# A Strassen-form FFN on one core: the order of its down preparation, and who makes its token block sums

## The chip, the cores and the metric

The kernel runs on one core of one Trainium2 chip. The core has TensorE (matmul; in the profile PE for matmuls, PEld for weight loads), VectorE (DVE), ScalarE (ACT), GpSimd (POOL) and SyncE (SP), which issues the DMAs. The metric is the time in microseconds (us) of one execution on the device; lower is better.

## The reference

One encoder layer is applied to two independent inputs of 1024 tokens x 1024 channels, with the same weights, and in the kernel the first input's pass ("trunk" 0) runs ahead of the second's (trunk 1). Only the FFN matters here:

```python
x = norm_1(h); h = h + concat(attention(x), rg_lru(x)) @ w_out     # w_out 1024 x 1024
xn = rms_norm(h, norm_ffn_g)
g, u = split(xn @ w_gate_up)          # w_gate_up 1024 x 5632
h = h + (silu(g) * u) @ w_down        # w_down 2816 x 1024
y = rms_norm(h, final_norm_g)         # meta tokens dropped
```

All is float32.

## The kernel before

**Exact products from rounded ones.** A float32 operand is split into a high part, its cast to float32r (ScalarE), and a low part, the operand minus its high part (VectorE or GpSimd). A product is then three matmuls (`mm3`): high x high, high x low, low x high.

**Seven products instead of eight.** Gate/up and down are computed in the Strassen-Winograd form: tokens, inner dimension and outputs are cut in two, and seven products of sums of blocks take the place of eight. So ahead of the matmuls stand block sums of the operands, and behind them additions of the results.

**Block sums of the tokens** (`x_side`, `sums`). The normalised token tiles `x2n` are taken in four blocks q of 2 x 128 tokens. Block q has quarters b11, b21, b12, b22, and needs T3 = b22 - b12, T1 = b12 - b11 and T2 = b22 - T1 = T3 + b11. T2 and T3 lie in the tile `t23` ("t" in the trace), T1 overwrites b12 (in `x2n`). TensorE transposes the blocks into PSUM (`tp`), ScalarE and VectorE split them into `xB`, `xT`, `xH`. For blocks 0 to 2 GpSimd makes all sums, for block 3 VectorE. `x_side` is a generator that is stepped between pieces of the output projection (`op`), while the last tiles of `h` are made and normalised: an ACT square, two small GpSimd operations (`ms`, `rs`) and one VectorE multiply for each tile.

**The down stage.** For each trunk it has seven products in the order P1, P2, P4, P5, P7, P6, P3, each in NC = 11 units of 12 matmuls (`dn_unit`): four token blocks q by three matmuls, into four PSUM banks that a product fills over its 11 units. A unit needs two operand tiles `wop`: `sop` (activations, tiles aA, aB, aC, aD, aS, aV) and `top` (weights, tiles `wraw` from HBM or `trun`). `prep_dn` makes the sums that its product asks for and ScalarE's two casts; `prep_dn_lo` makes the two low parts, that of `top` on VectorE and that of `sop` on GpSimd. Of sums, P1 and P3 have none; P2 and P7 have one on VectorE; P5 has two on VectorE; P4 has one on VectorE and one whose engine alternates (VectorE for even units, GpSimd for odd ones), besides a copy on ScalarE; P6 has one on VectorE and two of which one is VectorE's and one GpSimd's.

Operand tiles come from a ring of seven slots, so that at unit n the units n, n+1 and n+2 may hold tiles. Raw weight tiles have four slots; `load` issues the DMA of an item on SyncE's queue when the item four places ahead of it was given up by its low part (`freed`).

Every engine executes its instructions in the order in which the program issues them. For each unit n, `prep(n)` is issued first: the low parts of unit n+1 (`lows(n + 2)`), then sums and casts of unit n+2, then `lows(n + 1)`, which finds nothing left in the steady state. Then come the unit's matmuls, with at most two additions of the product before, `h += bank`, which VectorE reads from PSUM (`h<-h,dn` in the trace): after blocks q = 1 and q = 3, until the list `adds` is empty. A product leaves 16, 4, 4, 8, 8, 12 or 4 additions, in the order of the products. Behind trunk 0's P3 the first steps of trunk 1 are mixed in.

All instructions are recorded in the helper at L118, so the rows below are told apart by their tiles.

Of the kernel before, what the change touches and what calls it, by code (L numbers as in the profile page):

```python
# [12 lines left out]
ALU = mybir.AluOpType  # L13
# [23 lines left out]
NC = NHT // 2  # L37
# [207 lines left out]
def hymba_kernel(ctx, tc, ins, outs, dbg=None):  # L245
    nc = tc.nc
    plan = Plan()
    pe, act, dve, pool = (Engine(e, k, plan) for e, k in (
        (nc.tensor, "pe"), (nc.scalar, "act"), (nc.vector, "dve"), (nc.gpsimd, "pool")))
# [6 lines left out]
    def slot(tag, shape, dt=F32, name=None):  # L256
        if tag == "rope":
            return sm.tile(shape, dt, tag=tag, name=name, bufs=1)
        return sb.tile(shape, dt, tag=tag, name=name or tag)
# [168 lines left out]
    def mm3(out, lh, ll, rh, rl, first, last, more=False):  # L428

        pe.matmul(out, lhsT=lh, rhs=rh, start=first, stop=False, skip_group_check=more)  # L430
        pe.matmul(out, lhsT=lh, rhs=rl, start=False, stop=False, skip_group_check=more)
        pe.matmul(out, lhsT=ll, rhs=rh, start=False, stop=last, skip_group_check=more)
# [704 lines left out]
    def attention(T, b):  # L1137
# [324 lines left out]
        def x_alloc(n, tags, at=0, both=None):  # L1462
            tl = both if both is not None else slot(tags[0], [P, 2, 4, 512], F32R, name="x" + n)
            X[n] = (tl[:, 0], [(0, tl[:, 1])])

        def x_trans(n, q, src):
            tp = T.x_mk([P, 4, P], "tp")
            for i in range(4):
                pe.transpose(tp[:, i, :], src[:, i * P:(i + 1) * P], idf)
            hi, los = X[n]  # L1470
            qs = slice(q * P, (q + 1) * P)
            act.copy(hi[:, :, qs], tp)
            for k0, lo in los:
                k1 = k0 + lo.shape[1]
                dve.tensor_tensor(lo[:, :, qs], tp[:, k0:k1], fv(hi[:, k0:k1, qs]), ALU.subtract)
            T.x_in[n] += 1

        def x_side():
            t23 = {}

            def blocks(q):
                e, o = x2[2 * q], x2[2 * q + 1]
                return e[:, :512], e[:, 512:], o[:, :512], o[:, 512:]

            def sums(q, eng):
                b11, b21, b12, b22 = blocks(q)
                t23[q] = slot((S_CH, S_CL, "s6", "s2")[q], [P, 2, 512], name="t23")
                eng.tensor_tensor(t23[q][:, 1], b22, b12, ALU.subtract)
                eng.tensor_tensor(b12, b12, b11, ALU.subtract)
                eng.tensor_tensor(t23[q][:, 0], b22, b12, ALU.subtract)  # L1490

            def t4(q, eng):
                b21 = blocks(q)[1]
                eng.tensor_tensor(b21, t23[q][:, 0], b21, ALU.subtract)

            x_alloc("B11", T.xb[:1])
            x_alloc("T2", T.xb[1:])
            for q in range(3):
                while not {2 * q, 2 * q + 1} <= T.x2_done:
                    yield False  # L1500
                sums(q, pool)
                yield True
                x_trans("B11", q, blocks(q)[0])
                yield True
                x_trans("T2", q, t23[q][:, 0])
                yield True
            while not T.out_done:
                yield False
            x_alloc("B21", T.xa[:1])
            x_alloc("T3", T.xa[1:])  # L1510
            hi = slot("V", [P, 4, 512], F32R, name="xT1")
            X["T1"] = (hi, [(2 * i, slot(t, [P, 2, 512], F32R, name="xT1l")) for i, t in enumerate(("s7", f"wl{b}"))])
            for q in range(3):
                x_trans("T3", q, t23[q][:, 1])
                yield True
                x_trans("B21", q, blocks(q)[1])
                t4(q, pool)
                yield True
            while not {6, 7} <= T.x2_done:
                yield False  # L1520
            sums(3, dve)
            x_trans("B11", 3, blocks(3)[0])
            x_trans("T2", 3, t23[3][:, 0])
            x_trans("B21", 3, blocks(3)[1])
            t4(3, dve)
            T.x_go = True
            yield True
            x_trans("T3", 3, t23[3][:, 1])
            yield True
            for q in range(4):  # L1530
                x_trans("T1", q, blocks(q)[2])
                yield True
            hx = slot("H", [P, 2, 2, 4, 512], F32R, name="xH")
            x_alloc("T4", (), both=hx[:, 0])
            x_alloc("B22", (), both=hx[:, 1])
            for q in range(4):
                x_trans("T4", q, blocks(q)[1])
                yield True
            for q in range(4):
                x_trans("B22", q, blocks(q)[3])  # L1540
                yield True
# [54 lines left out]
        for _ in pvs:  # L1596
            pass
        pv_meta(7)
        T.side = x_side()
        for step in filler:  # L1600
            tick()
# [10 lines left out]
    def ffn_stream(T, b):  # L1612
# [12 lines left out]
        sums = {}  # L1625
# [29 lines left out]
        def load(limit=None):  # L1655

            while r_next[0] < len(items):
                i = r_next[0]
                if i >= 4 and items[i - 4][0] not in freed:
                    break  # L1660
                key, shape, parts = items[i]
                r = slot(raw_tags[i % 4], shape, name="wraw")
                for dst, src in parts:
                    sync.dma_start(out=dst(r), in_=src)
                raws[key] = r
                r_next[0] += 1
# [88 lines left out]
        def prep_dn_lo(p, c):  # L1755
            src, s, sop, top = half.pop((p, c))
            dve.tensor_tensor(top[:, 1], src, fv(top[:, 0]), ALU.subtract)
            pool.tensor_tensor(sop[:, 1], s, fv(sop[:, 0]), ALU.subtract)
            ops["dn", p, c] = (q4((sop[:, 0], sop[:, 1])), (top[:, 0], top[:, 1]))
            if p in ("P2", "P6", "P3"):  # L1760
                if c % 2 or c == NC - 1:
                    freed.add((p, c - c % 2))
            elif p in ("P4", "P5"):
                freed.add((p, c))
# [3 lines left out]
        def lows(n):  # L1768

            while n_lo[0] < min(n, T.n_prep2):  # L1770
                u = T.units[n_lo[0]]
                if u[0] == "dn":
                    prep_dn_lo(*u[1:])
                n_lo[0] += 1
            load()
# [3 lines left out]

        def prep(n):  # L1780

            lows(n + 2)
            while T.n_prep2 < len(T.units):
                u = T.units[T.n_prep2]
                need = 1 if u[0] == "gu" else 2
                out = sum(1 if x[0] == "gu" else 2 for x in T.units[n:T.n_prep2])
                if out + need > cap:
                    break
                if T.before_prep(u) is False:
                    break  # L1790
                (prep_gu if u[0] == "gu" else prep_dn)(*u[1:])
                T.n_prep2 += 1
                load()
            lows(n + 1)

        T.before_prep = lambda u: u[1:] == ("P1", 0)
        load()
        prep(0)
        T.prep_ops = prep

    def ffn(T, b, nxt):
# [9 lines left out]
        def bank(s, i, name):  # L1811
            tag = PB[s][i]
            return mk_d([P, 512], name) if tag is None else ps.tile([P, 512], F32, tag=tag, name=name)
# [113 lines left out]
        adds = []  # L1927
        banks = {}

        def add(p, q, i, l, sign, bk):  # L1930
            hs = T.h[:, 2 * q + i - 1, (l - 1) * 512:l * 512]
            dve.tensor_tensor(hs, hs, bk, ALU.add if sign > 0 else ALU.subtract)

        def dn_unit(p, c):
            n = DN.index(p)
            if c == 0:
                banks[n] = [bank(n % 2, q, "dn") for q in range(4)]
            (sh, sl), (th, tl) = ops.pop(("dn", p, c))
            for q in range(4):
                mm3(banks[n][q], sh[:, q], sl[:, q], th, tl, c == 0, c == NC - 1)  # L1940
                if q % 2 and adds:
                    adds.pop(0)()
            if c == NC - 1:
                assert not adds
                for q in range(4):
                    for i, l, sign in C[p]:
                        adds.append(lambda q=q, i=i, l=l, sign=sign, bk=banks[n][q]: (add(p, q, i, l, sign, bk), T.h_adds.add((p, q, i, l))))
# [212 lines left out]
```

## Time and profile before

| | us |
|---|---|
| median of 3 runs (lowest, highest) | 2554.81 (2551.83, 2556.84) |
| profiled execution | 2563.52 |
| its span, first to last instruction | 2561.7 |
| TensorE busy with matmuls / weight loads | 2385.7 / 2002.5 |
| VectorE / ScalarE / GpSimd busy | 1782.2 / 1168.3 / 1335.8 |
| mean granted TensorE clock | 0.97 |

Matmuls are pipelined, so a busy TensorE is not TensorE at its peak. Idle time of an engine costs something only where the chain that sets the end runs through it.

### The profile page before, as it was taken

How to read it: one execution, taken by the hardware profiler on the slowest of the kernel's cores; microseconds unless marked ns; L12 is line 12 of the kernel's file. 1: busy time of each engine (PE TensorE's matmuls, PEld its weight loads, DVE VectorE, ACT ScalarE, POOL GpSimd, SP SyncE). 2: the span in 40 equal slices, each digit the busy share in tenths (PEclk: the TensorE clock that was granted, in tenths of full speed). 3: DMA queues.
4: the chain of work that ended last, by engine and by line, in shares of the span. 5: the costliest groups of instructions: out<-in, count | busy, mean ns of one | idle time of the engine just before them, and what ended most of it. 6: DMA issues, size and time to landing. Idle time of an engine off the chain costs nothing.

```text
span 2561.7 us, 34088 instructions
## 1 busy us (share of the span) xinstructions
PE 2385.7 (93%) x12402; PEld 2002.5 (78%) x12402; DVE 1782.2 (70%) x2462; ACT 1168.3 (46%) x2083; POOL 1335.8 (52%) x1222
## 2 busy tenths in 40 slices
PE   7998999989999999998889889999799999999887
PEld 7878998867888888766677789988678888878665
DVE  6787888876555555778866778888665555557787
ACT  4456666654223232333535566666442222224434
POOL 5434766554444444445763356665544444444456
PEclk9998999989999999999999889999899999999999
DMA  5112000112222224741330130001122232247402
GB/s 137 37 35 101 19 17 18 42 66 65 76 78 82 88 74 156 271 148 38 136 128 19 35 108 18 9 18 42 66 66 74 83 91 74 83 159 276 149 30 111
DMA packets 189703, 212.77 MB, mean 83 GB/s; under 512 B 24272, under 2 KB 141008, under 8 KB 188512
## 3 DMA queue, kind: packets, MB, share of 16 engines
q1 hardware_dynamic: 189536, 210.60, 24.9%
q8 instruction: 98, 1.61, 0.3%
q14 instruction: 69, 0.57, 0.1%
HBM read 168.45 MB, written 39.85 MB: 81 GB/s over the span
## 4 chain that ended last, share of the span: by engine, by line
PE 65%; DVE 18%; ACT 6%; POOL 5%; issue 5%; DMA 1%; SPq 0%; ACTq 0%; DVEq 0%; POOLq 0%
PE gu L118 33%; PE op L118 5%; PE dn L118 5%; PE S L118 4%; PE pvo L118 4%; PE ptp L118 3%; DVE wop L118 3%; ACT wop L118 2%; PE pin L118 2%; PE qp L118 2%; DVE arena L118 2%; PE gp L118 2%; PE pg L118 1%; DVE m L118 1%; ACT arena L118 1%
## 5 line engine op out<-in xcount | busy, mean ns | idle before, releaser
L118 PE MATMUL dn<-wop 128*128 128x512 f32 x1848 | 463.4, 403 | 44.8 <-DVE wop L118 34.0
L118 PEld LDWEIGHTS dn<-wop 128*128 128x128 f32 x1848 | 340.7, 189 | 160.8 <-DVE wop L118 68.0
L118 PE MATMUL gu<-xT,wop 128*128 128x512 f32 x1408 | 371.2, 394 | 0.0
L118 POOL TENSOR_TENSOR pexp<-pexp,rsum 128x1024 f32<-128x1024 f32 x128 | 243.3, 1900 | 234.1 <-DVE rsum L118 150.7
L118 POOL TENSOR_TENSOR wop<-wraw,wop 128x512 fp32r<-128x512 f32 x176 | 230.7, 1311 | 217.0 <-ACT wop L118 217.0
L118 POOL TENSOR_TENSOR wop<-wsum,wop 128x512 fp32r<-128x512 f32 x132 | 171.7, 1301 | 269.0 <-ACT wop L118 269.0
L118 PEld LDWEIGHTS gu<-xT,wop 128*128 128x128 f32 x1408 | 264.0, 188 | 59.4
L118 PE MATMUL gu<-xB,wop 128*128 128x512 f32 x1056 | 265.5, 399 | 2.9 <-DVE xB L118 2.9
L118 ACT CAST wop<-wraw 128x512 fp32r<-128x512 f32 x264 | 162.5, 616 | 229.3 <-DVE wraw L118 159.9
L118 PE MATMUL gu<-xH,wop 128*128 128x512 f32 x1056 | 254.7, 396 | 1.7 <-DVE act L118 1.7
L118 PEld LDWEIGHTS gu<-xH,wop 128*128 128x128 f32 x1056 | 198.7, 188 | 50.5 <-issue 2.5
L118 PEld LDWEIGHTS gu<-xB,wop 128*128 128x128 f32 x1056 | 199.5, 190 | 49.0 <-DVE xB L118 3.6
L118 ACT CAST pt<-ptp 128x512 fp32r<-128x512 f32 x256 | 149.1, 586 | 127.9 <-PE ptp L118 126.7
L118 DVE TENSOR_REDUCE m<-S 128x1 f32<-128x1041 f32 x128 | 158.2, 1236 | 52.7 <-PE S L118 51.9
L118 ACT ACTIVATE pexp<-S,m 128x1041 f32<-128x1041 f32 x128 | 145.0, 1133 | 57.8 <-DVE m L118 55.1
L118 DVE TENSOR_TENSOR pt<-ptp,pt 128x512 fp32r<-128x512 f32 x256 | 168.2, 682 | 3.4 <-ACT pt L118 2.2
L118 PE MATMUL ptp<-idf,pexp 128*128 128x128 f32 x1024 | 157.0, 278 | 11.8 <-DVE pt L118 6.7
L118 PE MATMUL pvo<-pt,vst 128*128 128x256 f32 x1024 | 155.3, 295 | 3.6 <-DVE attnT L118 3.5
L118 PE MATMUL S<-kh,qs 128*128 128x348 f32 (+1 forms) x384 | 136.6, 358 | 19.3 <-ACT pexp L118 9.8
L118 ACT CAST wop<-wsum 128x512 fp32r<-128x512 f32 x132 | 81.8, 620 | 141.8 <-DVE wsum L118 141.8
L118 DVE SCALAR_TENSOR_TENSOR act<-th,act 128x512 f32<-128x512 f32 x88 | 143.8, 1634 | 3.0
L118 PEld LDWEIGHTS ptp<-idf,pexp 128*128 128x128 f32 x1024 | 126.9, 144 | 22.5 <-issue 7.8
(290 smaller groups left out, 5246.3 us busy)
## 6 DMA issues: line engine op xcount, KB each, us to landing
wraw<-in_w_gate_up SPq DMA_DIRECT2D x176, 256.0 KB, 3.5
wraw<-in_w_down SPq DMA_DIRECT2D x110, 256.0 KB, 2.8
ad<-act SPq DMA_DIRECT2D x44, 512.0 KB, 3.5
wraw<-in_w_down SPq DMA_DIRECT2D x22, 512.0 KB, 3.2
wraw<-in_w_in SPq DMA_DIRECT2D x32, 256.0 KB, 3.3
hd<-h SPq DMA_DIRECT2D x16, 512.0 KB, 5.1
h<-hd SPq DMA_DIRECT2D x16, 512.0 KB, 10.7
out<-h SPq DMA_DIRECT2D x15, 512.0 KB, 2.7
```

The lines of the kernel that those rows point to most:

```text
L118: return fn(*args, **kw)
```

## The change

Three edits. `sums`: the first difference T3 and the update of b12 are made by VectorE for each block, and T2 is made as T3 + b11 between them, by VectorE for blocks 0 and 3 and by GpSimd for blocks 1 and 2. `prep`: the low parts of unit n+1 are issued after the sums and casts of unit n+2 instead of ahead of them. `dn_unit`: the additions of the product before are spread over all 11 units of the present one, except in P3.

```diff
             def sums(q, eng):
                 b11, b21, b12, b22 = blocks(q)
                 t23[q] = slot((S_CH, S_CL, "s6", "s2")[q], [P, 2, 512], name="t23")
-                eng.tensor_tensor(t23[q][:, 1], b22, b12, ALU.subtract)
-                eng.tensor_tensor(b12, b12, b11, ALU.subtract)
-                eng.tensor_tensor(t23[q][:, 0], b22, b12, ALU.subtract)
+                dve.tensor_tensor(t23[q][:, 1], b22, b12, ALU.subtract)
+                eng.tensor_tensor(t23[q][:, 0], t23[q][:, 1], b11, ALU.add)
+                dve.tensor_tensor(b12, b12, b11, ALU.subtract)
...
-                sums(q, pool)
+                sums(q, (dve, pool, pool)[q])
...
         def prep(n):
 
-            lows(n + 2)
             while T.n_prep2 < len(T.units):
...
-            lows(n + 1)
+            lows(n + 2)
...
+            due = -(-len(adds) // (NC - c)) if p != "P3" else min(2, len(adds))
             for q in range(4):
                 mm3(banks[n][q], sh[:, q], sl[:, q], th, tl, c == 0, c == NC - 1)
-                if q % 2 and adds:
+                if q % 2 and due:
+                    due -= 1
                     adds.pop(0)()
```

## Rows read from the trace of the kernel before

**Rows 1.** The page, busy time by engine over the whole span.
```profile
PE 2385.7 (93%) x12402; PEld 2002.5 (78%) x12402; DVE 1782.2 (70%) x2462; ACT 1168.3 (46%) x2083; POOL 1335.8 (52%) x1222
```
**Rows 2.** Windows of trunk 1's P2, P4, P5, P7, P6: length, busy (instructions), granted clock, DMA.
```profile
2327.47:2359.33 31.86, 31.86 (x139) 25.82 (x138) 30.69 (x40) 12.77 (x23) 14.26 (x11) 1.00 0.59 231
2359.33:2400.74 41.41, 37.30 (x146) 26.40 (x144) 28.12 (x33) 17.65 (x32) 22.83 (x16) 1.00 0.40 140
2400.74:2436.93 36.19, 33.57 (x132) 23.97 (x132) 28.37 (x37) 13.58 (x22) 14.27 (x11) 1.00 0.46 160
2436.93:2472.72 35.79, 33.42 (x132) 23.97 (x132) 27.18 (x33) 12.66 (x22) 15.21 (x12) 1.00 0.00 1
2472.72:2514.73 42.01, 32.59 (x124) 22.40 (x124) 39.03 (x41) 15.04 (x25) 35.66 (x22) 1.00 0.20 69
```
**Rows 3.** Timeline of P2: start, duration, instruction; two low parts of VectorE.
```profile
2339.30 1.05 DVE L118 TENSOR_TENSOR wop<-wraw,wop 128x512 fp32r<-128x512 f32 x1
...
2342.08 1.03 DVE L118 TENSOR_TENSOR wop<-wraw,wop 128x512 fp32r<-128x512 f32 x1
```
**Rows 4.** Timeline of one unit of P7.
```profile
2442.08 1.43 DVE L118 TENSOR_TENSOR wop<-trun,wop 128x512 fp32r<-128x512 f32 x1
2443.43 0.68 DVE L118 TENSOR_TENSOR aD<-aA,aD 128x512 f32<-128x512 f32 x1
...
2444.20 0.62 ACT L118 CAST wop<-aD 128x512 fp32r<-128x512 f32 x1 [2.15 <-DVE aD L118]
2444.72 0.62 ACT L118 CAST wop<-trun 128x512 fp32r<-128x512 f32 x1
2444.95 1.30 POOL L118 TENSOR_TENSOR wop<-aD,wop 128x512 fp32r<-128x512 f32 x1 [1.99 <-ACT wop L118]
2445.38 1.42 DVE L118 TENSOR_TENSOR wop<-trun,wop 128x512 fp32r<-128x512 f32 x1
```
**Rows 5.** Timeline of one unit of P5: its two sums, and the first of the next.
```profile
2403.95 0.68 DVE L118 TENSOR_TENSOR aC<-aD,aC 128x512 f32<-128x512 f32 x1
...
2404.55 0.68 DVE L118 TENSOR_TENSOR wraw<-wraw 128x512 f32<-128x512 f32 x1
...
2407.24 0.68 DVE L118 TENSOR_TENSOR aC<-aD,aC 128x512 f32<-128x512 f32 x1
```
**Rows 6.** Timeline of an odd unit of P4: both of its sums.
```profile
2374.69 0.68 DVE L118 TENSOR_TENSOR wraw<-wraw 128x512 f32<-128x512 f32 x1
...
2375.51 1.29 POOL L118 TENSOR_TENSOR wraw<-wraw,trun 128x512 f32<-128x512 f32 x1 [2.74 <-issue]
```
**Rows 7.** Timeline of P6: operations of GpSimd and VectorE that overlap.
```profile
2504.49 1.72 POOL L118 TENSOR_TENSOR wop<-aB,wop 128x512 fp32r<-128x512 f32 x1
2505.00 1.75 DVE L118 TENSOR_TENSOR aB<-aB 128x512 f32<-128x512 f32 x1
...
2506.17 1.74 POOL L118 TENSOR_TENSOR trun<-trun,wraw 128x512 f32<-128x512 f32 x1
```
**Rows 8.** Instructions of the tile dn: the additions, ns min/median/max.
```profile
L118 DVE TENSOR_TENSOR h<-h,dn x112: 672/675/683, 1057.3 to 2549.4; 128x512 f32<-128x512 f32 x112
```
**Rows 9.** Landing of wraw's loads from 2361 to 2438; DMA issues of h (median).
```profile
DMA to landing us min/median/max: 2.5/2.9/5.2
...
h<-hd SPq DMA_DIRECT2D x16, 512.0 KB, 10.7
```
**Rows 10.** Trunk 0's block sums: timeline of block 0; waits (total, times, longest); a window.
```profile
552.13 2.26 POOL L118 TENSOR_TENSOR t<-x2n 128x512 f32<-128x512 f32 x1 [0.95 <-DVE x2n L118]
...
556.67 1.26 POOL L118 TENSOR_TENSOR t<-x2n 128x512 f32<-128x512 f32 x1
...
557.99 1.02 PE L118 MATMUL tp<-idf,t 128*128 128x128 f32 x4 [4.01 <-POOL t L118]
...
PE tp L118 <- POOL t L118: 8.9, 3, 4.0
...
550.77:574.95 24.18, 14.74 (x61) 11.45 (x60) 16.52 (x18) 8.77 (x16) 21.36 (x20) 0.72 0.11 44
```

## The prediction, made before the changed kernel was run

> **What bounds the kernel now.** I read the page first. TensorE's matmuls are busy 93% of the span [rows 1], so only stretches in which TensorE waits have anything to give. The list of its waits shows two places that the change touches: the down product and the block sums ahead of the FFN.
>
> For the down product I cut the second trunk's stage at the end of the eleventh low part of each product that VectorE makes, and asked for the busy time in each piece; the first trunk repeats the lengths. P2 takes 31.9 us, P4 41.4, P5 36.2, P7 35.8, P6 42.0 [rows 2]. All have the same 132 matmuls to feed at the same granted clock, 1.00. In P2 the low parts follow one another every 2.78 us and TensorE never idles [rows 2, 3]: 2.78 us a unit, 30.6 for eleven, is TensorE's pace. The other four lose 10.8, 5.6, 5.2 and 11.4 us against it: 33 us a trunk.
>
> Why, I read in the timeline of one P7 unit [rows 4]. VectorE makes a low part at 2442.08, ending 2443.51, after GpSimd's own. Only then comes the sum for the next unit (2443.43), which was queued behind it. ScalarE's first cast waits for this sum (2444.20), its second cast runs behind the first (2444.72), and the next low part waits for that second cast (2445.38). The ring closes after 3.30 us: sum, cast, cast and low part stand in a row, and TensorE has no lead. P5 has the same ring with two sums, from 2403.95 to 2407.24: 3.29 us [rows 5]. In odd units of P4 a GpSimd sum is a further link (2375.51, behind VectorE's 2374.69) [rows 6].
>
> P6 is bound otherwise. A GpSimd operation begun at 2506.17 ends 1.16 us after VectorE's ended (2506.75 to 2507.91), and that one of VectorE ended 0.54 us after GpSimd's before it (2506.21) [rows 7]: when both read two SBUF tensors they take turns. The additions from PSUM never stretch (672 to 683 ns) [rows 8]. I call this the turn account: 0.60 us for a VectorE operation (0.60 apart in [rows 5], 0.54 behind GpSimd), 1.16 for one of GpSimd.
>
> **Sums and casts first.** The change moves VectorE's and GpSimd's sums of unit n+2 ahead of the low parts of n+1. ScalarE's casts keep their order, as do the DMAs among themselves; no operation goes away. A low part then has its casts behind it by a whole unit, and the ring opens. What is left is the larger of TensorE's 2.78 us and the turn account.
> - P7: sum, low part, GpSimd's low part: 2 x 0.60 + 1.16 = 2.36, under 2.78. So 30.6 us: gain 5.2.
> - P5: 3 x 0.60 + 1.16 = 2.96: 32.6 us, gain 3.6. With 0.54 for the turn behind GpSimd it is 2.90, gain 4.3.
> - P4: an even unit has three VectorE operations and one of GpSimd, an odd one two and two: 5 x 0.60 + 3 x 1.16 = 6.48 a pair, 3.24 a unit: 35.6 us, gain 5.8. GpSimd's sum now stands ahead of its low part of n+1 and waits for VectorE's sum; GpSimd idles from that sum's start to its own, 0.82 us [rows 6]. If no lead covers this, TensorE gets that low part up to 0.82 + 1.29 us later in five of eleven units, and the gain shrinks by up to 10 us, to nothing.
> - P6: three and two in each unit: 3 x 0.60 + 2 x 1.16 = 4.12, against 42.0 / 11 = 3.82 measured end to end. Both engines already take turns without a gap, so the order gives nothing: 0. At most it inherits a lead: in P7 the account leaves 2.78 - 2.36 = 0.42 a unit, and eleven of them, 4.6 us, could be spent here. I take none, and keep it for the lower bound.
> - P1 and P3 have no sums; P2 already runs at pace: 0.
> Sum: 14.6 us a trunk, 29 in all.
>
> The low part also releases a raw weight tile. On SyncE's queue the load keeps its place behind it, but the sum that reads it comes one unit earlier: the margin falls from about four units to three. Loads land in 2.9 us (longest 5.2) [rows 9]; three units are over 8 us. I cost this at nothing, and take it up below.
>
> **Additions spread out.** The same 56 additions a trunk, at most two a unit, now one in most. They read PSUM and stand outside the turn account. In P7, VectorE has 2 x 0.60 + 0.60 = 1.8 us of work instead of 2.4, under 2.78 either way. Their results are wanted only a product later. I take 0; if VectorE's own work were the limit, they would give at most 0.60 a unit in the first units of P5, P7 and P6, some 8 us over both trunks.
>
> **Block sums.** For block 0, GpSimd makes three in a row from 552.13 to 557.93, and TensorE waits 4.0 us for the last; over three blocks 8.9 us [rows 10]. Afterwards VectorE makes all three of block 0 and two of each of the next; GpSimd one each of blocks 1 and 2. Seven operations of GpSimd go, VectorE gets seven more of 0.60: 4.2 us. In the 24.2 us up to the last normalised tile GpSimd is busy 21.4 and VectorE 16.5 [rows 10], so VectorE becomes the fuller: 20.7 if it keeps its stretched durations. That allows 3.5 us; queueing behind the normalisations takes some. GpSimd's one sum waits for VectorE's difference, with the next tiles' normalisation factors queued behind it on GpSimd; before, they stood behind three sums. I take 2.8, plus 0.60 for the fourth block, whose sum for the transpose now comes second instead of third: 3.4 a trunk, 7 in all. Bounds: nothing, and the 8.9 waited for, cut by VectorE's load to 3.5 + 0.6 = 4.1.
>
> **Two rules of the Trainium skill.** Perfetto Trace Analysis, "Identifying the Most-Contended Engine", holds that matmul busy time misjudges TensorE's headroom and weight-load busy time shows it. In P7 matmuls are busy 33.42 of 35.79 us, so 2.4 would be to gain; weight loads 67% against 81% in P2 [rows 2], which gives 35.79 x (1 - 67/81) = 6.2. The spacing of the units gives 5.2, so the trace is nearer the rule. The same page, "Optimizing Scalar/DVE Operations", warns that work moved between GpSimd and VectorE may not help, as they share an SBUF read port. By it the block sums would gain 0 instead of 7 us.
>
> **Sum.** 29 + 7 = 36 us. The profiled run took 2563.5 us, its span 2561.7; it would fall to 2527. It stands 8.7 above the runs' median of 2554.8, and the gain scales by less than 1%, so I set 2519.
>
> **Rivals.**
> - Slower: the weight load comes too late. New order: low part of k, load, sums of k+4, low part of k+3: three units last at least the landing plus 1.8 us. At 2.9 that is 1.6 a unit, at 5.2 it is 2.3, both hidden. At 10.7, the landing of the h loads [rows 9], it is 4.2: P4 and P5 then lose 11 x (2 x 4.2 - 3.76 - 3.29) = 15 a trunk against 8.6 won in P7 and the block sums: 2567. It decides from about 10 us on. No load of these stretches comes near: 0.06.
> - No change: the casts stay late since their tiles come free late (the ring of seven), so sums made sooner don't help. Against it: P2 has the same ring and runs at pace [rows 3]. About 2555, 0.06.
> - Smaller gain: GpSimd's sum ahead of its low part eats P4's 5.8, and the block sums give nothing as in the rule above. Then P5 and P7, 8.8 a trunk, remain: 2537. VectorE's 28.1 to 28.4 busy us in P4 and P5 [rows 2] speak for such collisions: 0.25.
> - Larger gain: P6 gets the lead as well, block sums 4.1: 2 x (14.6 + 4.6 + 4.1) = 47: 2508 or less: 0.10.
> - The forecast, 2509 to 2530: 0.53.
>
> **The numbers.** 0.2% (5 us) is about what a measurement here tells from no change. Faster: 0.53 + 0.25 + 0.10 = 0.88; same 0.06; slower 0.06. The range runs from the larger gain with a little more (P5 at 2.90), 2503, to 5 us a trunk, 2544; it leaves out slower, no change and the tails of the others.
>
> **What would show it.** Low parts 2.8 us apart in P7, about 3.0 in P5, 3.2 in P4, 3.8 still in P6; in P7 ScalarE's casts running while VectorE makes the low part of the unit before; TensorE's 4.0 us wait for block 0 under 1.5. Wrong would be spacings of 3.3 with VectorE waiting for casts as now, loads waited for by sums, or VectorE full while the block sums wait.

## The result, and the profile after

The changed kernel takes 2519.28 us (median of four executions, 2518.87 to 2520.88), the kernel before 2555.82 on the same chip (four, 2551.83 to 2558.39): a ratio of 0.986, 95% interval 0.9842 to 0.9877, or 36.5 us less. The forecast was 2519. In the two profiled executions the span falls by more, from 2561.7 to 2517.6: the profiled execution of before took 2563.5 us, more than any other execution of that kernel here (2551.83 to 2560.5). The page of the changed kernel, busy time by engine, answers to [rows 1]:

```profile
PE 2357.4 (94%) x12402; PEld 1997.3 (79%) x12402; DVE 1814.0 (72%) x2476; ACT 1167.2 (46%) x2083; POOL 1328.6 (53%) x1208
```

Fourteen operations went from GpSimd to VectorE, seven a trunk. TensorE runs the same instructions in 28 us less busy time.

Now the windows of trunk 1, cut as in [rows 2] at the eleventh low part of VectorE in P2, P4, P5, P7 and P6; the columns are length, then busy time (instructions) of TensorE's matmuls and weight loads, VectorE, ScalarE, GpSimd, then granted clock, DMA share and GB/s:

```profile
2298.56:2329.79 31.23, 31.23 (x136) 25.32 (x135) 27.61 (x40) 13.09 (x23) 14.71 (x12) 1.00 0.57 215
2329.79:2366.11 36.32, 34.82 (x148) 27.28 (x147) 36.15 (x35) 18.41 (x33) 26.65 (x17) 1.00 0.48 159
2366.11:2396.87 30.76, 30.76 (x130) 23.43 (x129) 30.70 (x37) 13.66 (x23) 16.85 (x12) 1.00 0.57 184
2396.87:2428.91 32.04, 31.92 (x138) 25.54 (x136) 32.01 (x33) 12.88 (x22) 18.87 (x13) 1.00 0.05 15
2428.91:2469.53 40.62, 31.14 (x119) 21.61 (x120) 40.48 (x38) 12.74 (x21) 32.62 (x20) 1.00 0.19 64
```

P4, P5, P7 and P6 took 155.4 us, and take 139.7. The reader is to compare VectorE's column with the length: in P4 28.1 of 41.4 before, now 36.15 of 36.32. VectorE hardly waits any more (0.4 us over the four); it is executing, or held by GpSimd inside an operation that has begun. TensorE hardly idles in P5 and P7 and waits in P4 and P6.

A low part may be made early, so these cuts give a stage a lead that another spends. For all comparisons from here on I cut at the matmuls, from the first of a product's 132 to the first of the next product's. The same stretch of trunk 1 by that cut, first the kernel before (P4, P5, P7, P6), then the changed one:

```profile
2362.05:2400.21 38.16, 34.18 (x133) 24.20 (x132) 26.93 (x31) 16.62 (x30) 20.79 (x15) 1.00 0.39 138
2400.21:2436.33 36.12, 33.58 (x133) 23.97 (x132) 28.30 (x37) 13.58 (x22) 14.21 (x11) 1.00 0.46 160
2436.33:2472.52 36.19, 33.61 (x133) 23.97 (x132) 27.58 (x32) 12.66 (x22) 15.07 (x13) 1.00 0.00 1
2472.52:2516.68 44.16, 34.74 (x134) 23.94 (x133) 41.18 (x42) 15.04 (x25) 37.81 (x23) 1.00 0.19 66
```

```profile
2333.15:2366.11 32.96, 31.46 (x133) 24.58 (x132) 32.82 (x33) 16.75 (x30) 23.79 (x15) 1.00 0.48 159
2366.11:2397.75 31.64, 31.64 (x134) 24.14 (x133) 31.58 (x37) 13.66 (x23) 17.73 (x12) 1.00 0.56 183
2397.75:2428.39 30.64, 30.64 (x133) 24.82 (x132) 30.61 (x32) 12.88 (x22) 17.99 (x13) 1.00 0.02 5
2428.39:2472.56 44.17, 34.56 (x133) 24.04 (x132) 42.91 (x40) 13.88 (x23) 35.65 (x22) 1.00 0.19 63
```

P4 gains 5.2 us, P5 4.5, P7 5.5, P6 nothing: 15.2. Trunk 0 gives 15.6 by the same cut, so 30.8 in all, and 2.7 more in its P3.

How the ring opened is seen in P7, in the timeline of the changed kernel (start, duration, instruction, in brackets the idle time before it and what ended it); [rows 4] are the same unit before:

```profile
2402.39 1.56 DVE L118 TENSOR_TENSOR aD<-aA,aD 128x512 f32<-128x512 f32 x1
2403.87 0.68 DVE L118 TENSOR_TENSOR wop<-trun,wop 128x512 fp32r<-128x512 f32 x1
2404.03 0.62 ACT L118 CAST wop<-aD 128x512 fp32r<-128x512 f32 x1 [1.54 <-DVE aD L118]
2404.48 0.67 DVE L118 TENSOR_TENSOR h<-h,dn 128x512 f32<-128x512 f32 x1
2404.56 0.62 ACT L118 CAST wop<-trun 128x512 fp32r<-128x512 f32 x1
2404.79 1.30 POOL L118 TENSOR_TENSOR wop<-aD,wop 128x512 fp32r<-128x512 f32 x1 [1.39 <-ACT wop L118]
2405.07 1.56 DVE L118 TENSOR_TENSOR aD<-aA,aD 128x512 f32<-128x512 f32 x1
2406.56 0.68 DVE L118 TENSOR_TENSOR wop<-trun,wop 128x512 fp32r<-128x512 f32 x1
```

VectorE makes the low part (2403.87) right behind the next unit's sum, on casts that were ready; ScalarE casts that sum while the low part runs. Low parts come 2.69 us apart instead of 3.30. What is left is VectorE's own row: a sum that GpSimd's low part holds for 1.49 us (2405.07 to the start behind it at 2406.56, where 0.60 is the price of a free one), 0.61 for the low part, 0.59 for the addition. That is under TensorE's 2.78.

Of the DMAs, the instructions of tile `wraw` on SyncE's queue from P4 to P7 and their landing (least, median, longest) answer to [rows 9]:

```profile
L95 SPq DMA_DIRECT2D wraw<-in_w_down x33: 327/328/583, 2329.9 to 2395.0; - x33
...
DMA to landing us min/median/max: 2.5/3.1/4.8
```

Nothing in the stage waited for one. For the block sums, the waits of TensorE over both trunks (total, times, longest), first in the changed kernel, then before:

```profile
PE tp L118 <- POOL t L118: 18.4, 4, 5.9
...
PE tp L118 <- DVE t L118: 5.7, 4, 2.2
```

```profile
PE tp L118 <- POOL t L118: 17.9, 6, 4.0
...
PE tp L118 <- DVE t L118: 5.4, 2, 2.7
```

And the windows of trunk 0's stretch from the last attention matmul to the first of gate/up, in the same order:

```profile
547.86:581.43 33.57, 19.49 (x100) 15.61 (x99) 27.34 (x38) 14.99 (x27) 15.25 (x22) 0.84 0.08 32
```

```profile
546.94:583.74 36.80, 22.47 (x99) 17.91 (x99) 25.19 (x31) 14.82 (x27) 26.74 (x29) 0.74 0.07 29
```

The stretch is 3.2 us shorter (2.9 in trunk 1) and GpSimd's 26.7 busy us became 15.3, but TensorE waits for the sums as long as before: 24.1 us in all against 23.3. In trunk 0 the wait for block 0 falls from 4.0 us to 0.75, but those for blocks 1 and 2 grow from 2.9 and 2.0 to 5.9 and 3.3. By the windows TensorE's idle time in trunk 0 is as before (14.1 us against 14.3); what is shorter is its busy time with the same matmuls, 19.5 against 22.5, at a granted clock of 0.84 instead of 0.74. The timeline of trunk 0 shows why:

```profile
561.45 0.74 DVE L118 SCALAR_TENSOR_TENSOR h<-op,rs,h 128x512 f32<-128x512 f32 x1
562.11 0.68 DVE L118 TENSOR_TENSOR t<-x2n 128x512 f32<-128x512 f32 x1
...
562.87 1.77 POOL L118 TENSOR_TENSOR t<-t,x2n 128x512 f32<-128x512 f32 x1 [6.10 <-DVE t L118]
...
564.70 1.12 PE L118 MATMUL tp<-idf,t 128*128 128x128 f32 x4 [5.93 <-POOL t L118]
```

GpSimd, idle for 6.10 us, waits for VectorE's difference, which stood behind the output projection's additions and normalisations.

### The profile page after: what moved, and what is told of

It is laid out like the page before. It is cut to its first block, busy times and chain, and to the rows that moved or that the text cites. A ratio compares the mean times of both kernels' runs of the same rounds, so it can differ in the third digit from the quotient of the medians.

```text
span 2517.6 us, 34095 instructions
## 1 busy us (share of the span) xinstructions
PE 2357.4 (94%) x12402; PEld 1997.3 (79%) x12402; DVE 1814.0 (72%) x2476; ACT 1167.2 (46%) x2083; POOL 1328.6 (53%) x1208
## 4 chain that ended last, share of the span: by engine, by line
PE 66%; DVE 22%; ACT 4%; issue 4%; POOL 3%; DMA 1%; SPq 0%; DVEq 0%; POOLq 0%; ACTq 0%
PE gu L118 33%; PE dn L118 6%; PE op L118 6%; PE S L118 5%; PE pvo L118 4%; PE ptp L118 4%; DVE wop L118 3%; PE pin L118 2%; PE qp L118 2%; DVE arena L118 2%; DVE h L118 2%; DVE wraw L118 2%; PE gp L118 2%; PE pg L118 1%; PE tp L118 1%
## 5 line engine op out<-in xcount | busy, mean ns | idle before, releaser
L118 PE MATMUL dn<-wop 128*128 128x512 f32 x1848 | 448.3, 400 | 27.7 <-DVE wop L118 18.3
```

The lines of the kernel that those rows point to most:

```text
L118: return fn(*args, **kw)
```

## The experiments

All of them compute the whole reference. The first four take the change apart. Lengths by the matmul cut in trunk 1, us (trunk 0 agrees within 0.8):

| | P4 | P5 | P7 | P6 |
|---|---|---|---|---|
| before | 38.16 | 36.12 | 36.19 | 44.16 |
| changed | 32.96 | 31.64 | 30.64 | 44.17 |
| e1_order | 32.45 | 36.78 | 30.65 | 42.34 |
| e2_sums | 38.18 | 36.10 | 36.19 | 44.15 |
| e3_adds | 38.30 | 36.10 | 36.45 | 43.78 |
| e4_no_adds | 32.48 | 37.45 | 30.64 | 42.33 |
| e5_p6_low_first | 32.97 | 31.63 | 30.65 | 40.56 |
| e9_gap2 | 34.81 | 31.62 | 30.64 | 43.99 |
| e11_all_dve | 30.62 | 30.56 | 30.65 | 34.26 |

**e1_order: the new order alone.**

```diff
         def prep(n):
-            lows(n + 2)
             while T.n_prep2 < len(T.units):
...
-            lows(n + 1)
+            lows(n + 2)
```

> The kernel before with the new order of low parts alone. Theory (the ring of sum, cast, cast and low part was the limit, and the order opens it): the down stages shrink as in the changed kernel, P4 by about 5, P5 by 4.5, P7 by 5.5 us a trunk, so about 29 us less than before, and the stretch ahead of gate/up stays at 37 us from the last spa matmul to the first gu matmul. Rival (VectorE is simply too full, and the spreading of the additions made the room): well under 29, about 20 us less.

2523.26 us against 2556.27 on the same chip: 0.9875 (0.9861 to 0.9888), 33.0 us less. By the total the order carries nearly the whole gain; by the stages it carries less. The four products give 24.5 us over both trunks, of the changed kernel's 30.8, and trunk 0's P3 2.7; the rest came in stretches that the order does not touch (below, under what the sum leaves over). The table shows P5 unimproved, and P6 better than in the changed kernel.

**e2_sums: the block sums alone.**

```diff
-                eng.tensor_tensor(t23[q][:, 1], b22, b12, ALU.subtract)
-                eng.tensor_tensor(b12, b12, b11, ALU.subtract)
-                eng.tensor_tensor(t23[q][:, 0], b22, b12, ALU.subtract)
+                dve.tensor_tensor(t23[q][:, 1], b22, b12, ALU.subtract)
+                eng.tensor_tensor(t23[q][:, 0], t23[q][:, 1], b11, ALU.add)
+                dve.tensor_tensor(b12, b12, b11, ALU.subtract)
...
-                sums(q, pool)
+                sums(q, (dve, pool, pool)[q])
```

> The kernel before with the new block sums alone. Theory: about 3 us a trunk ahead of gate/up, 6 to 7 us less than before, the down stages as before. Rival (work moved between two engines that take turns gives nothing): no change, within 2 us.

2550.87 us, 0.9977 (0.9968 to 0.9986): 5.4 less, with 4 to 8 in the interval. The rival's 0 falls. In its trace the two front stretches are 3.2 and 3.7 us shorter, so the gain stands where the edit is.

**e3_adds: the additions spread, in the old order.**

```diff
+            due = -(-len(adds) // (NC - c)) if p != "P3" else min(2, len(adds))
...
-                if q % 2 and adds:
+                if q % 2 and due:
+                    due -= 1
                     adds.pop(0)()
```

> The kernel before with the additions spread out alone. Theory: they fill time in which VectorE waits for a cast or for GpSimd anyway, so within 3 us of before. Rival (VectorE's work is the limit): up to 8 us less.

2557.41 us, 1.0007 (0.9999 to 1.0016): nothing, as expected.

**e4_no_adds: the changed kernel without that edit** (order and block sums).

> The changed kernel with the additions as before, two a unit at the front. Theory: within 3 us of the changed kernel, 34 to 37 us less than before. Rival (in the new order VectorE is the fuller engine, so two additions in a unit now cost): 8 us slower than the changed kernel, seen in the first units of P5, P7 and P6.

2517.65 us, 0.9851 (0.9837 to 0.9864): by the total, as expected. By the stages it is not "nothing": P5 is 5.8 us longer than in the changed kernel (5.1 in trunk 0), P6 1.8 shorter, P4 0.5 shorter. They do not cancel: over both trunks the four products are 6.4 us longer, and stretches that no edit touches came out shorter in this program. The timeline of its P5 shows the 5.8 (here GpSimd's row covers four operations), and under it the first two of them by duration (least, median, most, ns):

```profile
2367.57 0.68 DVE L118 TENSOR_TENSOR wraw<-wraw 128x512 f32<-128x512 f32 x1
...
2368.17 0.68 DVE L118 TENSOR_TENSOR wop<-wraw,wop 128x512 fp32r<-128x512 f32 x1
...
2368.49 11.70 POOL L118 TENSOR_TENSOR wop<-aC,wop 128x512 fp32r<-128x512 f32 x4 [1.49 <-ACT wop L118]
2368.78 0.68 DVE L118 TENSOR_TENSOR aC<-aD,aC 128x512 f32<-128x512 f32 x1
...
2374.20 0.67 DVE L118 TENSOR_TENSOR aB<-aB 128x512 f32<-128x512 f32 x1
2374.96 1.58 DVE L118 TENSOR_TENSOR wraw<-wraw 128x512 f32<-128x512 f32 x1
...
2376.05 4.21 PE L118 MATMUL dn<-wop 128*128 128x512 f32 x9 [3.87 <-POOL wop L118]
```

```profile
L118 POOL TENSOR_TENSOR wop<-aC,wop x2: 1727/4620/7512, 2368.5 to 2376.0; 128x512 fp32r<-128x512 f32 x2
```

GpSimd's low part begins at 2368.49 and takes 7.51 us. In that time VectorE starts ten operations, from 2368.78 to 2374.20, each 0.60 behind the one before and none stretched. Only at a gap of VectorE (0.76 to the next start, 2374.96) does GpSimd get on, and that next operation of VectorE is the stretched one. In e1_order, trunk 1, VectorE had such a gap because it waited 0.17 us for a weight load. TensorE waits 3.87 us, and its granted clock over P5 falls to 0.91.

This happens once a trunk, here and in e1_order, each time in the first unit without an addition behind units with two (7.5, 7.5, 7.5 and 8.1 us). Bunched as two a unit, P4's four additions fill two units of P5 and then cease. In the changed kernel, with one addition in each of four units and then none, all seven low parts of this form take 1.51 to 1.52, with and without an addition in their unit. The start alone does not tell the cases apart: the low part that is shut out begins 0.31 us behind VectorE's, as those do that get their turn (2380.27 behind 2379.96 in the changed kernel, where VectorE's next operation is the one that stretches, to 1.79). What makes the lock pass in one and not in the other is open.

**e11_all_dve: the changed kernel with P4's to P6's sums and low parts all on VectorE.** Beside it the changed kernel ran once more on the same chip, as c0_changed.

```diff
-            turn = (dve, pool)[c % 2]
+            turn = dve
...
-                (pool, dve)[c % 2].tensor_tensor(A[1, 2, c], A[1, 2, c], A[1, 1, c], ALU.subtract)
+                dve.tensor_tensor(A[1, 2, c], A[1, 2, c], A[1, 1, c], ALU.subtract)
...
-            pool.tensor_tensor(sop[:, 1], s, fv(sop[:, 0]), ALU.subtract)
+            (pool if p in ("P1", "P2", "P3") else dve).tensor_tensor(sop[:, 1], s, fv(sop[:, 0]), ALU.subtract)
```

> The changed kernel again, beside the three below: 2517 to 2522 us.

> The changed kernel with every down sum on VectorE, and in P4, P5, P7 and P6 the low part of the activations on VectorE too, so that GpSimd does nothing there. Theory (the turn account of VectorE and GpSimd is what remains in P4, P5 and P6: 1.16 for an operation of GpSimd, 0.60 for the same on VectorE): VectorE's own work is 2.4 us a unit in P4 and P5, 1.8 in P7, 3.0 in P6, with additions 2.6, 2.6, 2.2 and 3.4; so from first matmul to first matmul P4 30.6 (33.0 now), P5 30.6 (31.6), P7 30.6, P6 about 38 (44.1): 9.7 a trunk, 19 us less than the changed kernel, about 2500. Rival (more work on VectorE makes it the limit, as it already waits for nothing but GpSimd): no gain, or slower than 2519.

c0_changed: 2518.99 us, 0.9855 (0.9842 to 0.9869). e11_all_dve: 2491.17, 0.9747 (0.9734 to 0.976): 27.8 us under the changed kernel where I expected 19, and every product but P6 at TensorE's pace. P6 took 34.3 us instead of the 38 expected, which is most of the difference. The windows of its P4, P5, P7 and P6:

```profile
2316.43:2347.05 30.62, 30.62 (x133) 24.80 (x132) 30.08 (x50) 17.26 (x31) 0.00 (x0) 1.00 0.57 191
2347.05:2377.61 30.56, 30.56 (x133) 24.81 (x132) 27.48 (x46) 12.97 (x22) 0.00 (x0) 1.00 0.51 171
2377.61:2408.26 30.65, 30.65 (x133) 24.80 (x132) 28.36 (x47) 12.57 (x22) 0.00 (x0) 1.00 0.06 18
2408.26:2442.52 34.26, 33.04 (x133) 24.39 (x132) 32.70 (x54) 13.28 (x22) 5.69 (x3) 1.00 0.20 69
```

VectorE has 14 to 17 more instructions in P4 and P6 than in the changed kernel and is busy for less time. An operation that costs 1.16 in turn costs 0.60 here. So it was the work shared with GpSimd, its turns and the pauses in which it waits for VectorE, that held P4 and P6, and no transfer or ring. The run takes both away and does not tell them apart.

**e13_all_dve_no_adds: the same without spreading the additions.**

```diff
-            due = -(-len(adds) // (NC - c)) if p != "P3" else min(2, len(adds))
...
-                if q % 2 and due:
-                    due -= 1
+                if q % 2 and adds:
```

> As the run above, with the additions as in the kernel before, two a unit at the front. Theory (in the new order the additions matter only because GpSimd gets its turn while VectorE reads PSUM: with four additions in P5's first two units VectorE then ran 1.8 us a unit and one low part of GpSimd took 7.5 us): without GpSimd in these products the 5 us lost in P5 are gone, P5 30.6, and the time is within 3 us of the run above. Rival (VectorE's work at the front of P5 is too much with two additions): P5 still above 35 us.

2492.89 us, 0.9751 (0.9738 to 0.9765), 1.7 from e11_all_dve with overlapping intervals, and P5 takes 30.56 us. With no GpSimd operation in P4 to P6 the place of the additions does not matter, as the reading of e4_no_adds has it.

**e10_block_dve and e12_all_dve_block: all block sums on VectorE**, on the changed kernel and on e11_all_dve.

```diff
-                sums(q, (dve, pool, pool)[q])
+                sums(q, dve)
```

> The changed kernel with all block sums on VectorE, none on GpSimd. Theory (an operation of GpSimd takes 1.7 us there in turns, and TensorE waits for it 5.9 and 3.3 us a trunk): T2 of blocks 1 and 2 comes about 1.2 us earlier each, VectorE gets 1.2 us more: 1 to 2 us a trunk less, 2516. Rival (VectorE is the full engine there, every operation more is paid): 1.2 us a trunk more, 2522.

> All down sums and, in P4 to P6, all low parts on VectorE, as in the run at 2491 us, and all block sums on VectorE too, which alone gave 1.4 us on the changed kernel. Theory (the two act at different places): 2489 to 2491 us. Rival: the block sums give nothing here, 2491 to 2493.

2517.59 us (0.985, 0.9837 to 0.9864), 1.4 under c0_changed, and 2487.33 (0.9727, 0.9712 to 0.9741), 3.8 under e11_all_dve, which ran on another chip; neither pair of intervals is apart, so a small gain is likely and not proved. In the traces the two front stretches together are 1.4 us shorter in e10_block_dve and 1.1 in e12_all_dve_block, so the edit accounts for no more than about that much of either total. e12_all_dve_block is the fastest version of this study, 69.6 us under the kernel before.

**e5_p6_low_first: in P6 alone the old order.**

```diff
         def prep(n):
+            if n < len(T.units) and T.units[n][:2] == ("dn", "P6"):
+                lows(n + 2)
```

> The changed kernel with the low parts ahead of the sums again in P6 alone. In P6 a pair of units now takes 8.6 us between low parts, 8.0 to 8.1 in the kernel before. Theory (the new order lets GpSimd stand still for a moment in every pair of P6): pairs of about 8.1 again, 11 x 0.25 = 3 us a trunk, some 5 us less than the changed kernel, if the lead that P7 leaves is kept: about 2514. Rival (the pair is slower because an addition now stands in each unit): pairs stay at 8.6, 2519.

2511.18 us, 0.982 (0.9805 to 0.9835), 8 under the changed kernel with the intervals apart, and P6 takes 40.56 us: 3.6 less than before and after, in trunk 1 (3.5 and 3.4 in trunk 0). The timelines of P6, in the changed kernel and then here, show the unit in which GpSimd has a sum:

```profile
2443.71 1.76 DVE L118 TENSOR_TENSOR wop<-trun,wop 128x512 fp32r<-128x512 f32 x1
2445.40 0.67 DVE L118 TENSOR_TENSOR h<-h,dn 128x512 f32<-128x512 f32 x1
...
2445.99 0.68 DVE L118 TENSOR_TENSOR aA<-aC,aA 128x512 f32<-128x512 f32 x1
...
2446.75 1.68 POOL L118 TENSOR_TENSOR aS<-aS,aA 128x512 f32<-128x512 f32 x1 [1.83 <-DVE aA L118]
```

```profile
2440.89 0.68 DVE L118 TENSOR_TENSOR aA<-aC,aA 128x512 f32<-128x512 f32 x1
...
2441.64 1.68 POOL L118 TENSOR_TENSOR aS<-aS,aA 128x512 f32<-128x512 f32 x1 [1.23 <-DVE aA L118]
```

GpSimd's sum waits for VectorE's. In the kernel before, the same pause stood in every second unit, as long as in e5_p6_low_first:

```profile
2502.84 1.68 POOL L118 TENSOR_TENSOR aV<-aV,aB 128x512 f32<-128x512 f32 x1 [1.23 <-DVE aB L118]
```

In the changed order an addition stands right ahead of that sum and lengthens GpSimd's pause by 0.60 us for each pair of units; in the old order it falls after it.

**e8_gap3 and e9_gap2: the weight loads later in the program**, to bring the rival of a late load nearer. A load's issue waits in the program for the item three (e8) or two (e9) places ahead instead of four.

```diff
-                if i >= 4 and items[i - 4][0] not in freed:
+                if i >= 4 and items[i - (2 if isinstance(items[i][0][0], str) else 4)][0] not in freed:
```

> The changed kernel with raw weight loads of the down stage issued when the item three places ahead is given up, instead of four: one more unit of margin gone, two units left. Theory (loads land in 3.1 us, 4.8 at the longest): 3.1 + 1.8 = 4.9 in two units, 2.45 a unit, hidden: 2519 within 3 us. Rival (the loads are at their limit in the new order): slower by 5 us and more, with sums waiting for loads in P4 and P5.

> The same with two places: one unit of margin. Theory (a unit must hold the landing and the sums and low part behind it): 3.1 + 1.8 = 4.9 us a unit in P4 and P5 instead of 3.0 and 2.9, about 40 us a trunk, 80 us slower than the changed kernel: 2600. Rival (loads are hidden by other means, as raw tiles are given up much earlier than they are needed): no change.

e8_gap3: 2513.81 us, 0.983 (0.9813 to 0.9846), no loss, the products as in the changed kernel. e9_gap2: 2520.03, 0.9856 (0.9842 to 0.9871), where I expected 2600: P5 stayed at 31.62, P4 lost 1.8, P2 3.0 (3.6 in trunk 0): about 9 us over both trunks, which the total hides, since the start of trunk 1 was 5 us shorter than in the changed kernel. My model of the load was wrong. By the code, the four raw slots were still there and a load still waits for its slot's former user, so what the edit moved was a load's place in SyncE's queue. It cost one long wait in P2 (P4's loss was not traced), in the list of VectorE's waits and in the chain of waits (start, length, what):

```profile
DVE trun L118 <- DMA wraw<-in_w_down: 5.4, 1, 5.4
```

```profile
2292.03 16.72 DMA wraw<-in_w_down
```

That load took 16.7 us while the DMA engines were nine tenths busy with the loads of `h` and the activations. In the changed kernel one of P2's loads takes 9.6 us and nobody waits. A version that really has fewer raw slots was not tried, so the landing time from which P4 and P5 would suffer stays open, and the rival of a late load is put aside by what the trace shows and not by a test.

## Why the prediction was right

**The ring, shown.** e1_order alone gives 24.5 of the 30.8 us in the four products (33.0 of 36.5 by the totals), and neither of the other two edits alone shortens them: e2_sums and e3_adds leave all four within 0.4 us in trunk 1. P7: 5.2 forecast, 5.5 measured, low parts 2.69 apart. That is under TensorE's 2.78, as in the sum, but not the account's 2.36: the addition in the unit takes time too. P4: 5.8 forecast, 5.2 measured; low parts 6.32 a pair instead of 6.48. The smaller-gain rival, GpSimd's sum ahead of its low part, can have taken no more than 0.6 us. P5: 3.6 forecast, or 4.3 at 2.90 a unit; the spacing is 2.90 and 4.5 is measured: the better of the two prices was right. Sum 14.6 forecast, 15.2 and 15.6 measured. The forecast was made with the cut at the low parts, and by that cut trunk 1's P4, P5, P7 and P6 gain 5.1, 5.4, 3.8 and 1.4: the sum is again right (15.7), its split among the products depends on the cut. Of the two ways to read TensorE's headroom in P7, the rule in the Trainium skill's Perfetto Trace Analysis, "Identifying the Most-Contended Engine", gave 6.2 from weight loads and the matmuls' busy time 2.4; the 5.5 measured bears the rule out. My first sentence, that only stretches in which TensorE waits have anything to give, does not hold as it is worded: of the 44 us between the two profiled executions, 28 came out of TensorE's busy time.

**P6, right by size and wrong by reason.** I took 0 because both engines "already take turns without a gap". They do not, and the account's own 4.12 a unit already stood above the 3.82 measured: before, GpSimd paused 1.23 us a pair for VectorE's sum (2502.84 above); the unit in [rows 7] is the other one of the pair. The zero is a gain and a loss. The lead from P7 is real, and e5_p6_low_first collects 3.6 of the 4.6 us that I kept for the bound; the new order together with the spread additions lengthens the pause to 1.83 and spends it.

**The additions, the step that failed.** "They read PSUM and stand outside the turn account. I take 0." For the order of before that holds (e3_adds). In the new order they cost 1.8 us in P6 and 0.5 in P4, and are worth 5.1 to 5.8 in P5 (the table's rows of e1_order and e4_no_adds against the changed kernel's), since without them a low part of GpSimd loses its turn for 6 us. That the totals are alike is no proof of the step: e4_no_adds got its 6.4 us back in stretches that no edit touches.

**The block sums.** 7 us forecast, 5.4 measured alone, 3.2 and 2.9 for the two stretches in the changed kernel. The size holds, the way does not: I expected TensorE's wait for block 0 to shrink to under 1.5 us, and it did (0.75), but the waits moved to blocks 1 and 2 with the same total. VectorE as the fuller engine, which I named as the limit, is what they now wait for. Which chain brought the 3 us is open. In trunk 0 nearly all of it is TensorE's busy time, at the higher granted clock (0.84 against 0.74); in trunk 1 it is 1.6 of the 2.9, at the same clock of 0.75. My account had no term for the clock, and whether it is a cause here or follows from where the waits fall is not shown. The last normalised tile comes 3.7 us earlier (24.3 us into the stretch instead of 28.0), but in e10_block_dve it comes 5.0 us earlier still, and the stretch is only 0.3 shorter (33.3, trunk 0). The rule of the Trainium skill that I weighed against it (Perfetto Trace Analysis, "Optimizing Scalar/DVE Operations": moving work between the two may not help, as they share a port) would have given 0; e2_sums measures 5.4, and e11_all_dve 28, nearly all of it in the down stage. An operation that moves to VectorE is not only relocated; it costs 0.60 in place of a turn of 1.16.

**The rivals.** Late weight loads: none was waited for, and the longest landed in 4.8 us; the tipping point itself was not reached. The ring of seven slots: refuted by the spacing of 2.69. The larger gain asked for P6's lead, which is there, but not in this kernel. One slip stands in the range: the larger gain with P5 at 2.90 is about 2507, not 2503. The result is far from either.

**What the sum leaves over.** Over the two profiled executions the down stages give 31.9 us (30.8 in the four products and 2.7 in trunk 0's P3, less 1.6 that trunk 1's P1 lost), the two front stretches 6.1, gate/up 2.0, and the start of trunk 1 up to its last attention matmul, which no edit touches, 5.0; the last 1 us goes the other way ahead of trunk 0's stretch: 44.0. The medians differ by 36.5, since the profiled execution of before stood 7.7 above its median. So the forecast's 36 is right to a few us, and its hitting the median within one is luck.

That untouched start of trunk 1 took 527 to 538 us over the programs of this study. By the traces, the order in which the engines execute its instructions differs between programs, and the length goes with it: 527.2, 527.2 and 528.7 in e1_order, e4_no_adds and e12_all_dve_block, which share one order; 531.7 to 533.0 in the changed kernel, c0_changed and three others, which share a second; 531.5 to 533.3 in e2_sums, e5_p6_low_first and e11_all_dve, which share a third with the kernel before. e8_gap3 (530.6) and e9_gap2 (527.9) have orders of their own. The profiled execution of the kernel before, with 537.7, stands alone; its mean granted clock there is 0.946, against 0.955 to 0.968 in the others. So some 5 us of e1_order's 33.0, and most of what e4_no_adds got back, come with another order in a stretch that was not edited. No group has one of the three edits in common that the others lack, so what picks the order is open. A stage's own length is the safer witness for differences of 5 us.

## What to carry to other kernels

In a queue that runs in order, issue what another engine waits for (here the sum that feeds the casts) ahead of what only TensorE wants a unit later: that alone gave 24.5 us in the four products, about 33 by the total. When VectorE and GpSimd work on the same tiles in SBUF, price an operation by what it takes of both engines: P6's operations on two engines took longer than all of them on VectorE alone (44.2 us against 34.3). And check an edit in the stage it touches; a total can hide a loss of 6 us behind a shorter stretch elsewhere.

## What the hardware showed that I had not expected

Taking turns is not fair. A GpSimd operation on two SBUF tensors that had begun, by the trace, made no headway while VectorE ran ten such operations back to back at their full pace of 0.60 us: it took 7.51 us, where the same operation takes 1.29 to 1.31 in P5 of the kernel before. It ended 1.2 us after a gap of 0.16 us in VectorE's row. The Trainium skill's SBUF — State Buffer, "Who interferes with whom", calls the ports that the two share an exclusive lock, and says that issue order decides who blocks. The stretched operations agree with the lock; this row does not agree with the order, since by the trace's starts GpSimd came first and ten later operations of VectorE went ahead.
